# Second parts of the weights by accumulating DMAs in a hybrid decoder trunk: input projections and branch outputs

## The chip, the cores and the metric

The kernel runs on one core of one Trainium2 chip. The metric is device time in microseconds: the median of the timed runs of one program. Each execution computes one layer for 512 tokens from inputs in HBM.

## The reference

Five token mixers run side by side on one normalised input; each has its own gate path, is projected to the model width, weighted by a sigmoid gate and summed:

```python
h = rmsnorm(x, norm_g)
proj = h @ w_in + b_in                      # 1024 -> 13320, split into 19 sections
y_a = silu(layernorm(conv31(a_val * sigmoid(a_glu)))) * silu(a_z)
y_b = stick_breaking_attention(b_q, b_k, b_v) * silu(b_z)
y_c = headnorm(mlstm_chunkwise(silu(conv4(c_q, c_k)), c_v, c_i, c_f)) * sigmoid(c_o) * silu(c_z)
y_d = rg_lru(conv4(d_x)) * silu(d_z)
y_m = memory_attention(m_q, rmsnorm(mem)) * silu(m_z)
gates = sigmoid(gate_logits)                # five of 512 x 1024
merged = sum(gates[n] * (y @ w_up[n]) for n, y in enumerate((y_a, y_b, y_c, y_d, y_m)))
return rmsnorm(x + merged @ w_out, final_norm_g)
```

All is in float32; x is 512 x 1024, each branch 512 wide, the memory 256 rows.

## The kernel before, in words

**Split matmuls.** TensorE multiplies float32r operands, which hold fewer bits than float32. So each operand is kept as two parts: a first part, the value rounded to float32r (`whi`, `hH`, `yH`), and a second part, what the rounding left (`wlo`, `hL`, `yL`). `mm3` (lines 193 to 201) then makes three matmuls a term: first by first (L199), first of the weights by second of the data (L200), second of the weights by first of the data (L201). They accumulate in one PSUM bank.

**Tiling.** The normalised input stands transposed in SBUF as `hH` and `hL`, 8 blocks of 128 channels by 512 tokens. One projection (`proj`, L203) computes 128 output channels for all 512 tokens: 8 terms, 24 matmuls. Its weights are one array of 128 x 1024 float32 (512 KB), worked on in two halves of 128 x 512, one for the first four terms and one for the last four. A branch output (`up`, L963) computes 128 of 1024 model channels with 4 terms, 12 matmuls; one weight load serves two of them, so a half is again 12 matmuls.

**Two ways to make the parts.** Both load the weights from HBM into a stage tile `wst` (two buffers) by a DMA issued from SyncE. `load_w` (L149) has ScalarE copy a half into `whi` (L162) and VectorE subtract: `wlo = wst - whi` (L163; L165 and L166 with a scale). `load_w_add` (L170) has ScalarE write the rounded negative into `wlo` (L182), GpSimd issue a DMA that reads the same half of the weights from HBM again and adds it onto `wlo` (L183), and ScalarE write `whi` (L184); VectorE has no part in it. `whi` and `wlo` have six buffers each (`WHL`), so that three weight loads are held at a time. Before, the 40 gate projections (step G) use `load_w_add`; all other projections, the branch outputs, the memory's keys and values and the token-major values (`v_half`) use `load_w`.

**Order of the work.** The list `STEPS` gives the steps in program order: ac, an, ao (convolution branch), ma (memory attention), bv, bp, ba (stick-breaking attention), cv, cg, cp, ch, cn (mLSTM), ds, dt, dn (RG-LRU), G (a gate) and U (a branch output). A scheduler then orders each engine's instructions by its own estimate of durations, with weight preparation moved up (`high_priority(offset=PREP)`, 201 places). Each engine runs its instructions strictly in the order so found. Ahead of the list stands a start stage: the memory's keys and values, the norm of x and its transposes (`x_T`, L317: `hH` L321, `hL` L322), with small tiles that are given free at its end; the memsets of `kp` (L544) on GpSimd wait for that. In a stick-breaking head (`b_head`) GpSimd masks scores (L611), VectorE scans them (L618) and TensorE transposes them (L628).

Of the kernel before, what the change touches and what calls it, by code (L numbers as in the profile page):

```python
# [18 lines left out]
D = 1024  # L19
# [13 lines left out]
GATES = 8200  # L33
# [4 lines left out]
CM_INDEX = {c: i for i, c in enumerate(CM)}  # L38
# [43 lines left out]
def build(ctx, tc, x, mem, memT, cols_d, rows_d, wcm, wbv, wcv0, wcv1, wmk, wmv, wup, wout, dw, fg, out):  # L82
# [26 lines left out]
    def col(name, i):  # L109
        o = _off[name] + i  # L110
        return cols[:, o:o + 1]
# [35 lines left out]
    def f32(t):  # L147
        return t.bitcast(F32)

    def load_w(src, n, scale=None, stage=wpool):  # L150

        st = stage.tile([P, 1056], F32, tag="wst", name="wst", bufs=WST)
        nc.sync.dma_start(out=st[:, :n], in_=src)
        res = []
        m = n // 2
        for half in range(2):
            hi = wpool.tile([P, 576], F32R, tag="whi", name="whi", bufs=WHL)
            lo = wpool.tile([P, 576], F32R, tag="wlo", name="wlo", bufs=WHL)
            f = st[:, half * m:(half + 1) * m]
            with tc.high_priority(offset=PREP):  # L160
                if scale is None:
                    act(hi[:, :m], f, AF.Copy)  # L162
                    V.tensor_tensor(out=lo[:, :m], in0=f, in1=f32(hi[:, :m]), op=ALU.subtract)  # L163
                else:
                    act(hi[:, :m], f, AF.Copy, scale=scale)  # L165
                    V.scalar_tensor_tensor(out=lo[:, :m], in0=f, scalar=scale, in1=f32(hi[:, :m]),  # L166
                                           op0=ALU.mult, op1=ALU.subtract)
            res.append((hi, lo))
        return res

    def load_w_add(src, n):

        st = wpool.tile([P, 1056], F32, tag="wst", name="wst", bufs=WST)
        nc.sync.dma_start(out=st[:, :n], in_=src)
        res = []
        m = n // 2
        for half in range(2):
            hi = wpool.tile([P, 576], F32R, tag="whi", name="whi", bufs=WHL)
            lo = wpool.tile([P, 576], F32R, tag="wlo", name="wlo", bufs=WHL)
            sl = slice(half * m, (half + 1) * m)  # L180
            with tc.high_priority(offset=PREP):
                act(lo[:, :m], st[:, sl], AF.Copy, scale=-1.0)  # L182
                G.dma_start(out=lo[:, :m], in_=src[:, sl], accum_op=ALU.add)  # L183
                act(hi[:, :m], st[:, sl], AF.Copy)  # L184
            res.append((hi, lo))
        return res

    def piece(w, k, n, per, o=0, c=None):

        hi, lo = w[k // per]  # L190
        sl = slice((k % per) * n + o, (k % per) * n + (o + c if c else n))
        return hi[:, sl], lo[:, sl]


    def mm3(ps, terms, first=True, last=True, check=False):

        n = len(terms)
        for i, (ah, al, bh, bl) in enumerate(terms):
            mm(ps, lhsT=ah, rhs=bh, start=first and i == 0, stop=False, skip_group_check=check)  # L199
            mm(ps, lhsT=ah, rhs=bl, start=False, stop=False, skip_group_check=check)  # L200
            mm(ps, lhsT=al, rhs=bh, start=False, stop=last and i == n - 1, skip_group_check=check)  # L201

    def proj(c, scale=None):  # L203

        w = load_w_add(wcm[CM_INDEX[c]], D) if c >= GATES else load_w(wcm[CM_INDEX[c]], D, scale)
        ps = pj.tile([P, S], F32, tag="pj", name="pj")
        mm3(ps, [(*piece(w, k, P, 4), hH[:, k, :], hL[:, k, :]) for k in range(NK)])
        return ps, col("b_in", CM_INDEX[c])
# [179 lines left out]
    def silu_proj(c):  # L388
        ps, b = proj(c)
        z = zt()  # L390
        silu_evac(ps, b, z)
        return z

    def split_proj(c, scale=None, bias=None):
        ps, b = proj(c, scale)
        hi, lo = op_pair()
        split_evac(ps, b if bias is None else bias, hi, lo)
        return hi, lo
# [4 lines left out]
    def a_conv(i):  # L403
        ps, b = proj(A_GLU + i * P)
        sg = tpool.tile([P, S], F32, tag="sg", name="sg")
        with tc.high_priority(offset=EVAC):
            act(sg, ps, AF.Sigmoid, bias=b)
        ps, b = proj(A_VAL + i * P)
        u = apool.tile([P, 30 + S], F32, tag="u", name="u")
        V.memset(u[:, :30], 0.0)  # L410
        with tc.high_priority(offset=EVAC):
            V.scalar_tensor_tensor(out=u[:, 30:], in0=ps, scalar=b, in1=sg, op0=ALU.add, op1=ALU.mult)
        a = apool.tile([P, S], F32, tag=f"acc{i}", name=f"acc{i}", bufs=1)
        V.tensor_scalar(a, u[:, 0:S], col("a_w", i * 31), col("a_b", i), op0=ALU.mult, op1=ALU.add)
        for k in range(1, 31):
            V.scalar_tensor_tensor(out=a, in0=u[:, k:k + S], scalar=col("a_w", i * 31 + k), in1=a,  # L416
                                   op0=ALU.mult, op1=ALU.add)
        acc[i] = a
# [530 lines left out]
    upw = {}  # L949
# [13 lines left out]
    def up(n, ys):  # L963
        d = ups[n]
        ups[n] += 1
        if d % 2 == 0:
            upw[n] = load_w(wup[n, d // 2], 1024)
        g = gates[n][d]
        ps = pj.tile([P, S], F32, tag="pj", name="pj")
        mm3(ps, [(*piece(upw[n], 4 * (d % 2) + k, P, 4), *ys[k]) for k in range(NE)])  # L970
        first = d not in begun
        begun.add(d)
        with tc.high_priority(offset=EVAC):
            V.tensor_tensor(out=merged[:, d, :] if first else g, in0=g, in1=ps, op=ALU.mult)
        if not first:
            V.tensor_tensor(out=merged[:, d, :], in0=merged[:, d, :], in1=g, op=ALU.add)
# [5 lines left out]
    def step(s):  # L982
# [17 lines left out]
        elif c == "ba":  # L1000
            p = st[f"bp{i // 2}"]
            b_head(p, i % 2)
            if s[:-1] + str(i ^ 1) in st:
                ys[1][i // 2] = y_split(p[4])
            st[s] = True
        elif c == "cv":
            c_v(i)
        elif c == "cg":
            c_gates()
        elif c == "cp":  # L1010
            st[s] = c_proj(i)
        elif c == "ch":
            st[s] = c_head(st[f"cp{i}"])
        elif c == "cn":
            ys[2][2 * i:2 * i + 2] = c_norm([st[f"ch{2 * i}"], st[f"ch{2 * i + 1}"]])
        elif c == "ds":
            d_setup()
        elif c == "dt":
            st[s] = d_tile(i)
        elif c == "dn":  # L1020
            ys[3][2 * i:2 * i + 2] = d_scan([st[f"dt{2 * i}"], st[f"dt{2 * i + 1}"]])
        elif c == "G":
            gate(i)
        elif c == "U":
            assert None not in ys[i]
            up(i, ys[i])
        else:
            raise ValueError(s)
# [43 lines left out]
    for half in range(2):  # L1072
        if half:
            wo = [hl for k2 in range(4) for hl in load_out(1, k2)]
        for t in range(NT):
            tsl = slice(t * P, (t + 1) * P)
            parts = parts_of(t) if half else 1
            w = S // parts
# [96 lines left out]
```

## Time and profile before

| | before |
|---|---|
| median of 3 runs | 839.41 us (838.4 to 839.54) |
| profiled execution: its time / its span | 838.62 us / 836.6 us |
| granted TensorE clock | 0.999 |
| TensorE busy | 825.4 us (99%) |
| VectorE, ScalarE, GpSimd busy | 572.6, 490.9, 104.7 us |
| DMA | 106.33 MB, mean 127 GB/s |

The span runs from the first to the last instruction; the execution's time has 2.0 us around it. A row of the page's groups names line, engine and operation, the tiles as out<-in, the count, then busy time and mean duration, then the engine's idle time just before these instructions and what ended it. A row of waits names who waited, for whom, the total, the count and the longest. Rows of the timeline begin with start and duration. PE is TensorE, DVE VectorE, ACT ScalarE, POOL GpSimd, SP SyncE; SPq, POOLq are their queues as issuers. A matmul's recorded duration is longer than the distance to the next one, since they are pipelined; the distances are read from starts.

### The profile page before, as it was taken

Reading aid. Unit: us, or ns where it says so; the run is one execution under the profiler, and the core shown is the slowest. Engines: PE = TensorE matmul, PEld = TensorE weight load, DVE = VectorE, ACT = ScalarE, POOL = GpSimd, SP = SyncE. Lnnn points to the kernel's source line nnn. Section 1 sums busy time; section 2 is a strip of 40 time slices with the busy share of each in tenths; the row PEclk is TensorE's granted clock in tenths of the full one; section 3 lists DMA queues with packets and bytes.
Section 4 is the critical chain, followed back from the end, with each engine's and each line's share of the span. In section 5 each row is a group of like instructions: output and inputs, shape, how many; then the busy total and the mean of one; then the engine's idle time right before and its main releaser. Section 6 shows DMA issues by size and latency. Waiting matters only on the chain.

```text
span 836.6 us, 11398 instructions
## 1 busy us (share of the span) xinstructions
PE 825.4 (99%) x4064; PEld 698.0 (83%) x4064; DVE 572.6 (68%) x1098; ACT 490.9 (59%) x892; POOL 104.7 (13%) x155
## 2 busy tenths in 40 slices
PE   8999999999999999999999999999999999999996
PEld 7788888888898889788888888888888888888886
DVE  4879989997456677785676778559657564535644
ACT  6644475635545554667556546586465977884424
POOL 0000020101100232022333000010000201120000
PEclk9999999999999999999999999999999999999999
DMA  9432274345624324336624243474352645685602
GB/s 358 153 128 99 88 153 112 103 125 129 154 95 124 92 89 101 109 96 139 149 90 119 84 139 101 128 170 105 98 142 76 140 121 141 141 180 162 213 34 101
DMA packets 36240, 106.33 MB, mean 127 GB/s; under 512 B 4052, under 2 KB 4180, under 8 KB 36184
## 3 DMA queue, kind: packets, MB, share of 16 engines
q1 hardware_dynamic: 23800, 83.06, 30.0%
q0 software_dynamic: 11520, 20.98, 15.3%
q10 hardware_dynamic: 864, 1.57, 0.5%
q8 instruction: 32, 0.52, 0.3%
q14 instruction: 24, 0.20, 0.1%
HBM read 103.49 MB, written 2.11 MB: 126 GB/s over the span
## 4 chain that ended last, share of the span: by engine, by line
PE 94%; ACT 2%; DVE 1%; DMA 1%; issue 1%; SPq 0%; ACTq 0%
PE pj L201 26%; PE pj L199 26%; PE pj L200 26%; PE pj L530 2%; PE pj L528 2%; PE pj L529 2%; PE po L642 1%; PE wb L628 1%; PE og L833 1%; PE mk L286 1%; PE zb L599 1%; PE zb L598 1%; DMA mt<-in 1%; PE tp L502 0%; DVE hL L322 0%
## 5 line engine op out<-in xcount | busy, mean ns | idle before, releaser
L201 PE MATMUL pj<-hH,wlo 128*128 128x512 f32 x768 | 299.9, 391 | 0.2 <-DVE wlo L163 0.2
L200 PE MATMUL pj<-hL,whi 128*128 128x512 f32 x768 | 299.8, 390 | 0.0
L199 PE MATMUL pj<-hH,whi 128*128 128x512 f32 x768 | 299.6, 390 | 0.1
L162 ACT ACTIVATE whi<-wst 128x512 fp32r<-128x512 f32 (+1 forms) x172 | 107.1, 631 | 163.1 <-PE pj L200 118.3
L201 PEld LDWEIGHTS pj<-hH,wlo 128*128 128x128 f32 x768 | 144.2, 188 | 30.4 <-DVE wlo L163 0.7
L199 PEld LDWEIGHTS pj<-hH,whi 128*128 128x128 f32 x768 | 144.2, 188 | 29.7 <-ACT g L960 0.5
L200 PEld LDWEIGHTS pj<-hL,whi 128*128 128x128 f32 x768 | 144.3, 188 | 29.4
L163 DVE TENSOR_TENSOR wlo<-wst,whi 128x512 fp32r<-128x512 f32 (+1 forms) x172 | 117.1, 687 | 74.4 <-ACT whi L162 74.2
L183 POOL DMA_DIRECT2D wlo<-in x80 | 69.5, 869 | 559.8 <-ACT wlo L182 424.6
L416 DVE SCALAR_TENSOR_TENSOR acc<-u,cols,acc 128x512 f32<-128x512 f32 x120 | 88.7, 747 | 1.4
L184 ACT ACTIVATE whi<-wst 128x512 fp32r<-128x512 f32 x80 | 50.3, 629 | 57.1 <-PE pj L200 41.2
L200 PE MATMUL pj<-yL,whi 128*128 128x512 f32 x160 | 62.5, 390 | 0.0
L199 PE MATMUL pj<-yH,whi 128*128 128x512 f32 x160 | 62.4, 391 | 0.0
L201 PE MATMUL pj<-yH,wlo 128*128 128x512 f32 x160 | 62.3, 390 | 0.0
L182 ACT ACTIVATE wlo<-wst 128x512 fp32r<-128x512 f32 x80 | 49.4, 618 | 5.9 <-PE at L529 4.0
L201 PEld LDWEIGHTS pj<-yH,wlo 128*128 128x128 f32 x160 | 30.1, 188 | 6.2
L199 PEld LDWEIGHTS pj<-yH,whi 128*128 128x128 f32 x160 | 30.0, 188 | 6.1
L200 PEld LDWEIGHTS pj<-yL,whi 128*128 128x128 f32 x160 | 30.1, 188 | 5.9
L618 DVE TENSOR_TENSOR_SCAN kp<-kp 128x512 f32<-128x512 f32 (+3 forms) x32 | 26.9, 859 | 10.8 <-POOL kp L611 10.6
L529 PE MATMUL pj<-wlo,hH 128*128 128x256 f32 (+1 forms) x112 | 31.8, 284 | 0.0
L530 PE MATMUL pj<-whi,hL 128*128 128x256 f32 (+1 forms) x112 | 31.8, 284 | 0.0
L528 PE MATMUL pj<-whi,hH 128*128 128x256 f32 (+1 forms) x112 | 31.5, 283 | 0.0
(310 smaller groups left out, 1232.4 us busy)
## 6 DMA issues: line engine op xcount, KB each, us to landing
wst<-in SPq DMA_DIRECT2D x136, 512.0 KB, 3.4
wlo<-in POOLq DMA_DIRECT2D x80, 256.0 KB, 5.3
xt<-in SPq DMA_DIRECT2D x4, 512.0 KB, 9.0
merged<-in SPq DMA_DIRECT2D x4, 512.0 KB, 3.2
wst<-in SPq DMA_DIRECT2D x2, 528.0 KB, 4.3
mr<-in SPq DMA_DIRECT2D x2, 512.0 KB, 10.7
f<-crow SPq DMA_DIRECT2D x4, 256.0 KB, 6.6
out<-merged SPq DMA_DIRECT2D x4, 256.0 KB, 2.0
```

What stands on the lines that cost most here:

```text
L162: act(hi[:, :m], f, AF.Copy)
L163: V.tensor_tensor(out=lo[:, :m], in0=f, in1=f32(hi[:, :m]), op=ALU.subtract)
L182: act(lo[:, :m], st[:, sl], AF.Copy, scale=-1.0)
L183: G.dma_start(out=lo[:, :m], in_=src[:, sl], accum_op=ALU.add)
L184: act(hi[:, :m], st[:, sl], AF.Copy)
L199: mm(ps, lhsT=ah, rhs=bh, start=first and i == 0, stop=False, skip_group_check=check)
L200: mm(ps, lhsT=ah, rhs=bl, start=False, stop=False, skip_group_check=check)
L201: mm(ps, lhsT=al, rhs=bh, start=False, stop=last and i == n - 1, skip_group_check=check)
L416: V.scalar_tensor_tensor(out=a, in0=u[:, k:k + S], scalar=col("a_w", i * 31 + k), in1=a, op0=ALU.mult, op1=ALU.add)
L528: mm(dst[t], lhsT=hH[:, k, tsl], rhs=wh, start=first, stop=False, skip_group_check=True)
L529: mm(dst[t], lhsT=hH[:, k, tsl], rhs=wl, start=False, stop=False, skip_group_check=True)
L530: mm(dst[t], lhsT=hL[:, k, tsl], rhs=wh, start=False, stop=k == NK - 1, skip_group_check=True)
```

## The change

Two conditions. Every projection without a scale, and every branch output, now takes its weights by `load_w_add`:

```diff
     def proj(c, scale=None):
 
-        w = load_w_add(wcm[CM_INDEX[c]], D) if c >= GATES else load_w(wcm[CM_INDEX[c]], D, scale)
+        w = load_w_add(wcm[CM_INDEX[c]], D) if scale is None else load_w(wcm[CM_INDEX[c]], D, scale)
         ps = pj.tile([P, S], F32, tag="pj", name="pj")
...
         if d % 2 == 0:
-            upw[n] = load_w(wup[n, d // 2], 1024)
+            upw[n] = load_w_add(wup[n, d // 2], 1024)
         g = gates[n][d]
```

Of 56 projections that are no gates, the 4 of `B_Q` have a scale and stay; 52 change. Of branch outputs there are 40, with 20 loads. That is 72 loads or 144 halves; with the gates 112 loads are then made so. The start stage and `v_half` stay with `load_w`. The scheduler orders all engines anew.

On ScalarE, at the end of the start stage. `wlo_484` and `whi_483` are the first half of the first projection (`A_GLU`, 0), the next pair its second half; `v` is the memory's values, `hH` the last two blocks of the transposed input. Before:

```order
L217 ACTIVATE v_420<-mkf_442 128x512
L162 ACTIVATE whi_483<-wst_481 128x512
L162 ACTIVATE whi_487<-wst_481 128x512
L357 ACTIVATE v_421<-mv_151,rsq_t_426 128x512
L357 ACTIVATE v_421<-mv_152,rsq_t_426 128x512
L321 ACTIVATE hH_106<-tp_383,cols_80 128x512
```

Now:

```order
L217 ACTIVATE v_420<-mkf_442 128x512
L182 ACTIVATE wlo_484<-wst_481 128x512
L182 ACTIVATE wlo_489<-wst_481 128x512
L184 ACTIVATE whi_483<-wst_481 128x512
L184 ACTIVATE whi_488<-wst_481 128x512
L357 ACTIVATE v_421<-mv_151,rsq_t_426 128x512
L357 ACTIVATE v_421<-mv_152,rsq_t_426 128x512
L321 ACTIVATE hH_106<-tp_383,cols_80 128x512
```

Two pieces have become four, the two lo-writes first; the values and `hH` follow two places later.

On ScalarE, in the first pair of RG-LRU tiles (steps dn0 and the gates, outputs and projections around it). `whi_6733` and `whi_6737` are a branch output's weights, `whi_6758` to `whi_6800` those of the projections `D_X` and `D_Z` after it. Before:

```order
L162 ACTIVATE whi_6737<-wst_6731 128x512
L939 ACTIVATE f_6383<-f_6383 128x512
L162 ACTIVATE whi_6758<-wst_6756 128x512
L960 ACT_TABLE_LOAD
L960 ACTIVATE g_6675<-pj_6650,cols_80 128x512
L217 ACTIVATE yH_6588<-f_6577 128x512
L162 ACTIVATE whi_6762<-wst_6756 128x512
L217 ACTIVATE yH_6595<-f_6580 128x512
L162 ACTIVATE whi_6796<-wst_6794 128x512
```

Now (`whi_6862` for 6737, `whi_6884` for 6758, `whi_6889` for 6762, `whi_6924` for 6796):

```order
L184 ACTIVATE whi_6862<-wst_6855 128x512
L182 ACTIVATE wlo_6863<-wst_6855 128x512
L184 ACTIVATE whi_6884<-wst_6882 128x512
L182 ACTIVATE wlo_6885<-wst_6882 128x512
L960 ACT_TABLE_LOAD
L960 ACTIVATE g_6799<-pj_6774,cols_80 128x512
L217 ACTIVATE yH_6712<-f_6701 128x512
L217 ACTIVATE yH_6719<-f_6704 128x512
L184 ACTIVATE whi_6889<-wst_6882 128x512
L182 ACTIVATE wlo_6890<-wst_6882 128x512
L184 ACTIVATE whi_6924<-wst_6922 128x512
L182 ACTIVATE wlo_6925<-wst_6922 128x512
```

The sequence is the same, with a lo-write behind each `whi`.

On GpSimd, the masks of the third stick-breaking head. Before:

```order
L611 AFFINE_SELECT kp00_474<-kp00_474 128x128
L611 AFFINE_SELECT f_3051<-f_3051 128x128
L611 AFFINE_SELECT kp01_476<-kp01_476 128x128 x2
L611 AFFINE_SELECT f_3064<-f_3064 128x128 x2
L611 AFFINE_SELECT kp02_479<-kp02_479 128x128
```

Now, with the two DMAs of a branch output's weights inside it:

```order
L611 AFFINE_SELECT kp00_474<-kp00_474 128x128
L183 DMA wlo_3345<-in_11 128x512
L183 DMA wlo_3350<-in_11 128x512
L611 AFFINE_SELECT f_3109<-f_3109 128x128
L611 AFFINE_SELECT kp01_476<-kp01_476 128x128 x2
```

The masks after the first now wait until the two DMAs ahead of them can be issued.

## The prediction

> **What bounds the kernel now.** I read the page first (busy shares and groups), then TensorE's waits, then the groups by stretches of 20 us, then the tile `wlo`, and at last the timeline at two places. The page's first line and the list of all that TensorE waits for settle most of it:
>
> ```profile
> PE 825.4 (99%) x4064; PEld 698.0 (83%) x4064; DVE 572.6 (68%) x1098; ACT 490.9 (59%) x892; POOL 104.7 (13%) x155
> ```
>
> ```profile
> PE mk L286 <- DVE mt L274: 1.8, 2, 1.0
> PE warm L241 <- POOL ident masks.py:199: 1.4, 1, 1.4
> PE tp L320 <- DVE hL L322: 1.1, 1, 1.1
> PE pj L201 <- DVE wlo L163: 0.2, 1, 0.2
> PE mk L286 <- ACT mt L276: 0.2, 1, 0.2
> ```
>
> TensorE waits 4.7 us in all of 836.6. The change touches the origin of one of these waits: 0.2 us at the first projection. So what it takes off VectorE cannot come back as time, unless something else is hidden there; what it adds behind a matmul can cost. The costs of each step are in the groups:
>
> ```profile
> L201 PE MATMUL pj<-hH,wlo 128*128 128x512 f32 x768 | 299.9, 391 | 0.2 <-DVE wlo L163 0.2
> L162 ACT ACTIVATE whi<-wst 128x512 fp32r<-128x512 f32 (+1 forms) x172 | 107.1, 631 | 163.1 <-PE pj L200 118.3
> L163 DVE TENSOR_TENSOR wlo<-wst,whi 128x512 fp32r<-128x512 f32 (+1 forms) x172 | 117.1, 687 | 74.4 <-ACT whi L162 74.2
> L183 POOL DMA_DIRECT2D wlo<-in x80 | 69.5, 869 | 559.8 <-ACT wlo L182 424.6
> L182 ACT ACTIVATE wlo<-wst 128x512 fp32r<-128x512 f32 x80 | 49.4, 618 | 5.9 <-PE at L529 4.0
> ```
>
> and in the tile `wlo`, whose last line is min, median and max of an accumulating DMA from its issue to its landing:
>
> ```profile
> L183 POOL DMA_DIRECT2D wlo<-in x80: 844/862/1070, 105.4 to 766.1; - x80
> DMA to landing us min/median/max: 3.6/5.3/9.1
> ```
>
> **The change in numbers.** 52 projections and 20 output loads move from `load_w` to `load_w_add`: 72 loads, 144 halves. Off VectorE go 144 x 687 ns = 99 us (573 to 474). ScalarE gets 144 x 618 ns = 89 us (491 to 580, 69% of the span). GpSimd gets 144 x 869 ns = 125 us (105 to 230, 27%). Removing VectorE's work is worth nothing but the 0.2 us above. ScalarE and GpSimd stay far from full on average, so the average gives "no change"; what matters is how late a second part now is, at each place.
>
> **The delay of one half, and its cover.** Before, a second part follows its first by one VectorE instruction (0.69 us). After, it takes a ScalarE write (0.62), a step from ScalarE's end to GpSimd's issue, and 5.3 us to landing. The step is 0.3 us, from a gate of today (666.56 + 0.61 = 667.17, issue at 667.47):
>
> ```profile
> 666.56 0.61 ACT L182 ACTIVATE wlo<-wst 128x512 fp32r<-128x512 f32 x1
> ...
> 667.47 0.87 POOL L183 DMA_DIRECT2D wlo<-in  x1 [2.96 <-ACT wlo L182]
> ```
>
> So a half comes later by about 0.62 + 0.3 + 5.3 - 0.69 = 5.5 us. The cover is the ring of six halves. An ordinary stretch of 20 us (columns: PE, PEld, DVE, ACT, POOL busy, clock, DMA share, GB/s):
>
> ```profile
> 200.00:220.00 20.00, 20.00 (x90) 16.54 (x90) 11.99 (x20) 10.82 (x20) 3.42 (x4) 1.00 0.58 139
> ```
>
> TensorE does 90 matmuls in it, 0.22 to 0.23 us each; a half has 12, 2.7 us. A half may be written when its predecessor in the ring has been read, five halves (13.6 us) ahead of its first use. ScalarE does wait for exactly that release:
>
> ```profile
> ACT whi L162 <- PE pj L200: 118.3, 75, 3.6
> ACT whi L184 <- PE pj L200: 41.2, 30, 2.9
> ```
>
> With `whi` first (0.63) that leaves 13.6 - 0.63 - 0.62 - 0.3 - 5.3 = 6.8 us to spare after the change, or 3.0 with the slowest landing. So wherever ScalarE still waits for TensorE, I cost the change at nothing; the cover is this slack. It is absent in two places, and thin in a third.
>
> **First place: the first projection.** There is no ring ahead of it yet; its weights arrive as it begins.
>
> ```profile
> 34.76 1.16 ACT L162 ACTIVATE whi<-wst 128x512 fp32r<-128x512 f32 x2 [0.23 <-DMA wst<-in]
> ...
> 37.92 0.51 PE L201 MATMUL pj<-hH,wlo 128*128 128x512 f32 x1 [0.23 <-DVE wlo L163]
> ```
>
> ScalarE was held by the load itself until 34.76, which the change does not touch. By the order, `wlo_484` is now ScalarE's first piece there: done at 34.76 + 0.62 = 35.4, issued at 35.7, landed at 35.7 + 5.3 = 41.0. TensorE's order puts the first matmul with it third in the projection, as before, so it waits from 37.9 to 41.0: **+3.1 us**. Bounds with the shortest and longest landing: 39.3 (+1.4) and 44.8 (+6.9). Everything after is delayed, since nothing later has slack to give back to a TensorE that is always busy. The second half is issued 0.87 us behind, and needed 14 matmuls (3.2 us) after the first: covered. The four ScalarE pieces instead of two push `hH` for the last two terms back by 1 to 2 us; those terms now come after the stall: covered. GpSimd's `kp` memsets wait for the start stage to close,
>
> ```profile
> 39.90 0.20 POOL L544 MEMSET kp<- 128x1 f32 x4 [38.28 <-DVE v L358]
> ```
>
> and now stand ahead of the second projection's DMAs; those are issued near 40 and needed about 10 matmuls after the second half's start, near 46: just covered.
>
> [...]
>
> **Second place: ScalarE is full.** The same view, from 640 us on:
>
> ```profile
> 640.00:660.00 20.00, 20.00 (x93) 16.55 (x92) 13.98 (x23) 17.15 (x26) 2.18 (x3) 1.00 0.33 94
> 660.00:680.00 20.00, 20.00 (x90) 16.55 (x89) 9.86 (x14) 19.69 (x29) 3.02 (x4) 1.00 0.65 143
> 680.00:700.00 20.00, 20.00 (x90) 16.57 (x89) 14.22 (x23) 9.85 (x18) 1.72 (x2) 1.00 0.51 139
> ```
>
> Here ScalarE does RG-LRU's functions with their table loads, and has 0.3 us left of 20. The change adds lo-writes of 0.53 us each (the pitch: two take 1.16, less 0.63). Ahead of this stretch come six new ones, 3.2 us, against an idle time of 2.5 us:
>
> ```profile
> 647.49 0.68 ACT L920 ACTIVATE f<-dps,cols 64x512 f32<-64x512 f32 x1 [2.49 <-PE dps L919]
> ```
>
> so ScalarE enters 0.7 us late (between 0 and 2). Then, where the next projections' first parts are written today, and where their first matmul with a second part stands:
>
> ```profile
> 676.28 0.62 ACT L162 ACTIVATE whi<-wst 128x512 fp32r<-128x512 f32 x1
> ...
> 679.55 0.62 ACT L162 ACTIVATE whi<-wst 128x512 fp32r<-128x512 f32 x1
> ...
> 681.87 0.62 ACT L162 ACTIVATE whi<-wst 128x512 fp32r<-128x512 f32 x1
> ```
>
> ```profile
> 683.15 0.39 PE L201 MATMUL pj<-yH,wlo 128*128 128x512 f32 x1
> ...
> 683.83 0.39 PE L201 MATMUL pj<-hH,wlo 128*128 128x512 f32 x1
> ```
>
> The change from `yH` to `hH` marks the first half's use, 683.83; the following halves are used at 686.55 and 689.27, by 2.72 us. After the change two lo-writes stand ahead of the first of these, three ahead of the second, four ahead of the third. Their second parts land at (start + shift + 0.62 + 0.53 for its own write + 0.3 + 5.3): 676.28 + 1.06 + 6.75 = 684.1 (0.3 late); 679.55 + 1.59 + 6.75 = 687.9 (1.3 late); 681.87 + 2.12 + 6.75 = 690.7 (1.5 late). With 0.7 from ahead the worst is 2.2 us late. The stalls don't add, since each one gives the next half as much: **+2.2 us**, between 0 (an order that keeps ScalarE ahead) and 4.5 (2 us late at entry, landing 1 us slower).
>
> **Third place: the stick-breaking heads.** GpSimd masks the scores that VectorE scans, and VectorE waits for it in all eight heads:
>
> ```profile
> DVE kp L618 <- POOL kp L611: 10.6, 8, 6.0
> ```
>
> In two more heads than before a pair of accumulating DMAs now stands between the masks of one head, 2 x 0.86 = 1.7 us. Two heads already have such rows today and TensorE waits for neither, so some cover is there: +0.4 us, between 0 and 3.4.
>
> **Sum.** 3.1 + 2.2 + 0.4 = 5.7 us. The profiled execution took 838.6 us (span 836.6); that makes 844.3, and its time is 0.8 under the median of the three runs (839.4), so the median after should be **845.1 us**.
>
> **Rivals.** (1) *Nothing shows.* Landings at the low end (3.6 us) and ScalarE's order absorbing the rest. The start then costs 1.4 us, 840.8 in the median, which is within 0.2% (1.7 us, about what a measurement of this kernel can tell from no change). For it: ScalarE's 118 us of waiting, two loaded heads without a wait. Against: at the start the median landing decides and 39.3 is the earliest. It is certain only at a landing of 2.2 us (35.7 + 2.2 = 37.9), under which nothing is lost at the start. Chance 0.15, and 0.02 of it for a landing a microsecond under any of today's, 2.6 us: 0.4 us at the start and nothing later, 839.8. [...]
>
> (2) *The DMA engines become the bound.* From these rows
>
> ```profile
> q1 hardware_dynamic: 23800, 83.06, 30.0%
> q0 software_dynamic: 11520, 20.98, 15.3%
> ```
>
> an accumulating DMA takes 0.153 x 836.6 / 80 = 1.60 us of all 16 engines, a plain load of 0.524 MB 0.300 x 836.6 / 83.06 x 0.524 = 1.58. A weight then needs 1.58 + 3.20 = 4.8 us of DMA per 5.45 us of TensorE (24 matmuls of 0.227 us), 88% in every dense stretch; over the run 30 + 15.3 x 224/80 = 73%. It decides where an accumulating DMA takes over 1.93 us. At 30% longer (2.08) each of 112 weights costs 0.3 us, +34 us, 873. For it: landings up to 9.1 us today. Against: the share above already holds the contention of today. Chance 0.10.
>
> (3) *Faster.* Even if all that VectorE's waits cost TensorE after 20 us went (1.1 + 0.2), that is 1.3 us and not measurable; something unseen would be needed. Chance 0.04.
>
> My forecast has 0.71, and of it a little lies under the bound: faster 0.04, same 0.16, slower 0.80. The range takes the ends of the three terms: 1.4 above the median (840.8) to 6.9 + 4.5 + 3.4 = 14.8 above (854.2); I take 840.4 to 856, leaving the rest of rival 1 below and rival 2 above.
>
> **What would show it.** TensorE's waits should name `wlo` by DMA: one near 38 us of 2 to 4 us, a few near 684 to 692, ScalarE without idle time from 640 to 690, and no DMA share over 0.95 in whole stretches of 20 us. The groups should show L163 at x28, L182 at x224. I am wrong if TensorE does not wait at the first projection, if most of the loss comes from ordinary stretches (200 to 260 us, say), or if the landing's median passes 7 us.

## The result, and the profile after

The changed kernel took **847.62 us** (median of 3 runs, 846.35 to 847.75) against 839.41 before: a ratio of 1.0097, with a 95% interval from 1.0074 to 1.0120. That is 8.2 us slower; 845.1 was forecast, in a range from 840.4 to 856.0. The profiled execution spans 845.5 us, 8.9 more than before's 836.6.

The busy line of the page after can be held against the prediction's sums for VectorE, ScalarE and GpSimd (474, 580 and 230 us). GpSimd's holds. VectorE fell by 82 us instead of 99, and ScalarE rose by 72 instead of 89: the sums took full durations, and neighbouring instructions of one engine overlap in the rows (two lo-writes of 0.62 us take 1.15):

```profile
PE 830.5 (98%) x4064; PEld 699.4 (83%) x4064; DVE 490.2 (58%) x954; ACT 562.8 (67%) x1036; POOL 229.7 (27%) x299
```

TensorE is 5 us *busier* with the same 4064 matmuls. Part of that is matmuls that ran slower, which a list of waits cannot show. The whole list of TensorE's waits after:

```profile
PE pj L201 <- DMA wlo<-in: 4.0, 3, 2.6
PE warm L241 <- POOL ident masks.py:199: 1.4, 1, 1.4
PE tp L320 <- DVE hL L322: 1.1, 1, 1.1
PE mk L286 <- DVE mt L274: 0.8, 1, 0.8
PE pj L199 <- ACT mH L217: 0.3, 1, 0.3
PE og L833 <- ACT wlo L182: 0.2, 1, 0.2
PE mk L286 <- ACT mt L276: 0.2, 1, 0.2
PE pj L199 <- DVE g L974: 0.2, 1, 0.2
```

The 0.2 us for VectorE's `wlo` at the first projection became 4.0 us for the DMA's `wlo`, in three waits. The first, in the timeline of TensorE (start, duration, instruction, and in brackets the idle time before it):

```profile
36.84 0.40 PE L200 MATMUL pj<-hL,whi 128*128 128x512 f32 x1
39.85 0.63 PE L201 MATMUL pj<-hH,wlo 128*128 128x512 f32 x1 [2.62 <-DMA wlo<-in]
40.28 0.63 PE L199 MATMUL pj<-hH,whi 128*128 128x512 f32 x1
...
43.26 0.49 PE L200 MATMUL pj<-hL,whi 128*128 128x512 f32 x1
43.60 0.39 PE L201 MATMUL pj<-hH,wlo 128*128 128x512 f32 x1
```

From 39.85 to 43.26 the matmuls start 0.43 us apart instead of 0.23. The stretches of that time (PE, PEld, DVE, ACT, POOL busy, granted clock, DMA share, GB/s) name the reason: the clock fell behind the pause, to 0.57 from 40 to 44 us (1.00 in before).

```profile
40.00:44.00 4.00, 4.00 (x11) 3.15 (x12) 0.75 (x1) 2.61 (x6) 1.71 (x5) 0.57 0.99 206
44.00:48.00 4.00, 4.00 (x19) 3.27 (x19) 0.00 (x0) 0.60 (x2) 1.07 (x2) 1.00 1.09 249
```

The other two waits for `wlo` stand in the RG-LRU stage:

```profile
690.02 0.50 PE L201 MATMUL pj<-hH,wlo 128*128 128x512 f32 x1 [0.47 <-DMA wlo<-in]
...
694.00 0.50 PE L201 MATMUL pj<-hH,wlo 128*128 128x512 f32 x1 [0.92 <-DMA wlo<-in]
```

**Where the 8.9 us are.** Waits and slow matmuls together are seen in the distances between matmul starts. For each kernel I took from its trace the distance from each matmul to the next, less the median distance of its shape, summed by stretch of the program, less the same sum of the kernel before. The first row is after; the others are the experiments below. Each row is one execution, and not always a typical one: those of e2, e4, e6, e8 and e12 are the longest of their kernels, 0.6, 2.3, 0.8, 1.7 and 5.0 us over the median, and that of e9 is 1.1 under it.

```
us over before        0-20  20-60  60-500  500-600  600-720  720-780  780-end   sum
after                 -0.4   +4.0   -0.2     +2.1     +2.1     +0.1     +1.2    9.0
e1 first back         -0.3   +6.5   -0.1     +3.5     +0.9     +0.4     +0.3   11.3
e2 first alone        -0.2   +3.8   -0.1      0.0      0.0     +0.5      0.0    4.2
e3 ups back           -0.2   +3.8   -0.2      0.0     +3.3      0.0      0.0    6.9
e4 lo last            +1.4   +7.1   -0.2     +1.7     +2.0     +0.3     +2.4   14.8
e5 fill (+2.5 filled) +0.5   +0.2   -0.1     +1.0     +2.2      0.0     +0.6    7.0
e6 first 4 back        0.0    0.0   -0.2     +3.8     +1.8     +0.2     +1.4    7.1
e7 forty               0.0    0.0   -0.2      0.0      0.0     +0.3      0.0    0.1
e8 ScalarE alone      -0.3    0.0   +0.5     +2.0     +4.0     +0.7      0.0    7.1
e9 VectorE, first 4   -0.2    0.0   -0.1     -0.1     +2.2     +0.4     +1.5    3.9
e10 VectorE negates   +1.4   +7.4   -0.1     -0.1     +4.5     +0.3     +2.4   15.9
e11 most               0.0    0.0   -0.1     +0.3     +0.4     +0.2      0.0    1.0
e12 most, ScalarE      0.0    0.0   -0.1     +7.2     +2.0      0.0      0.0    9.2
```

The last column is of the whole program (it holds what the rounded columns leave). After loses at four places: the start (4.0), the mLSTM heads at 500 to 600 us (2.1), the RG-LRU stage (2.1) and the tail (1.2). Between 60 and 500 us, where 76 of the 144 new lo-writes stand, it loses nothing.

The rest of the signs. The groups show the move as forecast (L182 and L183 x224, L163 x28). The DMA's share should have stayed under 0.95 in whole stretches of 20 us; it is over that in three of them:

```profile
L182 ACT ACTIVATE wlo<-wst 128x512 fp32r<-128x512 f32 x224 | 138.4, 619 | 17.0 <-PE pj L529 7.7 <-DMA wst<-in 5.2 <-PE at L529 4.0
L183 POOL DMA_DIRECT2D wlo<-in x224 | 195.1, 878 | 526.8 <-ACT wlo L182 492.3 <-ACT rr L838 11.7 <-ACT sg L223 5.7
L163 DVE TENSOR_TENSOR wlo<-wst,whi 128x512 fp32r<-128x512 f32 (+1 forms) x28 | 18.7, 687 | 15.5 <-ACT whi L162 15.4
```

```profile
40.00:60.00 20.00, 20.00 (x82) 16.36 (x83) 7.32 (x11) 12.35 (x21) 8.14 (x11) 0.91 1.02 226
60.00:80.00 20.00, 20.00 (x96) 16.78 (x95) 18.56 (x29) 10.09 (x17) 5.72 (x7) 1.00 1.02 214
...
760.00:780.00 20.00, 20.00 (x90) 16.56 (x89) 5.17 (x8) 10.15 (x18) 6.06 (x7) 1.00 1.05 250
```

and the tile `wlo` gives the way of an accumulating DMA from issue to landing, 5.3 us in the median before:

```profile
DMA to landing us min/median/max: 3.6/5.8/8.9
```

The plain loads became slower too: a weight load of 512 KB lands 5.2 us after its issue in the median, 3.4 before.

### The profile page after: what moved, and what is told of

It is laid out like the page before. It is cut to its first block, busy times and chain, and to the rows that moved or that the text cites. A ratio compares the mean times of both kernels' runs of the same rounds, so it can differ in the third digit from the quotient of the medians.

```text
span 845.5 us, 11696 instructions
## 1 busy us (share of the span) xinstructions
PE 830.5 (98%) x4064; PEld 699.4 (83%) x4064; DVE 490.2 (58%) x954; ACT 562.8 (67%) x1036; POOL 229.7 (27%) x299
## 3 DMA queue, kind: packets, MB, share of 16 engines
q0 software_dynamic: 32256, 58.73, 41.8%
q1 hardware_dynamic: 23800, 83.06, 31.7%
HBM read 141.24 MB, written 2.11 MB: 170 GB/s over the span
## 4 chain that ended last, share of the span: by engine, by line
PE 82%; ACT 5%; issue 5%; DMA 4%; DVE 2%; POOL 1%; SPq 0%; POOLq 0%; ACTq 0%
PE pj L199 23%; PE pj L201 23%; PE pj L200 23%; PE pj L528 2%; PE pj L530 2%; PE pj L529 2%; DMA f<-crow 2%; DMA wlo<-in 1%; PE po L642 1%; DMA wst<-in 1%; PE wb L628 1%; ACT whi L184 1%; ACT wlo L182 1%; POOL wlo L183 1%; PE mk L286 1%
## 5 line engine op out<-in xcount | busy, mean ns | idle before, releaser
L183 POOL DMA_DIRECT2D wlo<-in x224 | 195.1, 878 | 526.8 <-ACT wlo L182 492.3
L184 ACT ACTIVATE whi<-wst 128x512 fp32r<-128x512 f32 x224 | 140.3, 629 | 141.9 <-PE pj L200 89.7
L182 ACT ACTIVATE wlo<-wst 128x512 fp32r<-128x512 f32 x224 | 138.4, 619 | 17.0 <-PE pj L529 7.7
L974 DVE TENSOR_TENSOR g<-g,pj 128x512 f32<-128x512 f32 x32 | 21.8, 681 | 31.9 <-PE pj L201 31.8
L529 PE MATMUL pj<-wlo,hH 128*128 128x256 f32 (+1 forms) x112 | 31.7, 284 | 0.0
L530 PE MATMUL pj<-whi,hL 128*128 128x256 f32 (+1 forms) x112 | 31.7, 284 | 0.0
L528 PE MATMUL pj<-whi,hH 128*128 128x256 f32 (+1 forms) x112 | 31.7, 284 | 0.0
L751 DVE TENSOR_SCALAR f<-u,cols 128x512 f32<-128x512 f32 x12 | 6.8, 564 | 36.2 <-ACT u L746 21.1
```

Source lines behind the costliest of these rows:

```text
L528: mm(dst[t], lhsT=hH[:, k, tsl], rhs=wh, start=first, stop=False, skip_group_check=True)
L529: mm(dst[t], lhsT=hH[:, k, tsl], rhs=wl, start=False, stop=False, skip_group_check=True)
L530: mm(dst[t], lhsT=hL[:, k, tsl], rhs=wh, start=False, stop=k == NK - 1, skip_group_check=True)
```

## The experiments

Two theories stood at the beginning. *Local*: the time is lost at a few places where a second part has no lead. *Traffic everywhere*: 144 more accumulating DMAs slow all transfers, and the loss goes with their number. Medians below are of 4 to 11 runs, each beside runs of the kernel before on the same chip (838.78 to 839.14 in the median).

### The start: first projection given back (e1), alone (e2), reordered (e4), pause filled (e5), first four given back (e6)

e1 edits line 205 of the kernel after:

```diff
-        w = load_w_add(wcm[CM_INDEX[c]], D) if scale is None else load_w(wcm[CM_INDEX[c]], D, scale)
+        w = load_w_add(wcm[CM_INDEX[c]], D) if scale is None and c != A_GLU else load_w(wcm[CM_INDEX[c]], D, scale)
```

> The kernel after, with the first projection's weights (both halves) split by VectorE again; the other 70 changed loads stay. Local theory (9 us lost at five places, of which 4.2 at the first projection: a wait of 2.6 us for the accumulating DMA, then nine matmuls at half clock, 0.2 us more each): the wait and the half clock both go, 847.6 - 4.2 = 843.4 us, granted clock 1.00 from 40 to 44 us. Rival, traffic everywhere (the loss is spread over the 224 accumulating DMAs through slower landings): two of 224 change, 847.5 us. Rival on the clock (the half clock comes from something else than the pause): the wait goes and the dip stays, 847.6 - 2.4 = 845.2 us.

Measured: **849.71 us** (845.07 to 851.59), 1.0117 (1.0094 to 1.0140). Both theories miss the median; the local one named 843.4. Two of the six executions took 845.1 and 845.8 us; the traced one took 850.3. The wait did go from the first projection, and came back larger at the second:

```profile
37.61 0.50 PE L201 MATMUL pj<-hH,wlo 128*128 128x512 f32 x1 [0.25 <-DVE wlo L163]
47.27 0.79 PE L201 MATMUL pj<-hH,wlo 128*128 128x512 f32 x1 [3.92 <-DMA wlo<-in]
```

and GpSimd's timeline shows when that projection's DMAs were issued, at 38.41 us:

```profile
38.41 1.89 POOL L183 DMA_DIRECT2D wlo<-in  x2 [36.79 <-DVE wlo L163]
```

Its first half was issued when the first projection had just begun and landed 8.8 us later. In the kernel after, the pause and the slow matmuls behind it delay the need for this half to 46.6 us; with them gone the need comes about 3.4 us earlier. The landing itself also took longer here, 8.8 us against 5.9 for the same half in after.

e2 edits the same line of the kernel before:

```diff
-        w = load_w_add(wcm[CM_INDEX[c]], D) if c >= GATES else load_w(wcm[CM_INDEX[c]], D, scale)
+        w = load_w_add(wcm[CM_INDEX[c]], D) if c >= GATES or c == A_GLU else load_w(wcm[CM_INDEX[c]], D, scale)
```

> The kernel before, with only the first projection's second parts by accumulating DMAs. Local theory: the whole cost of the start without anything else, a wait of 2.5 to 3.1 us and the half clock behind it, 839.4 + 4.2 = 843.6 us. Rival, traffic everywhere: 839.5 us, not to be told from before. Rival on the clock: the wait alone, 839.4 + 2.4 = 841.8 us.

Measured: **842.22 us**, 1.0036 (1.0024 to 1.0048), 3.4 us more than before; its trace has 3.8 at the start (the wait and the half clock) and 0.5 at most anywhere else. The start's whole cost needs only these two DMAs of the 144 new ones, which speaks against traffic everywhere. Two of the five executions, 841.1 and 841.3 us at a mean granted clock of 0.999, lie 2.3 and 2.6 us over before, about what the longer wait alone costs; the other three, at 0.995 to 0.997, lie 3.4 to 4.0 over it. So the half clock may follow the pause in some executions only. That isn't shown, as only one of them was traced.

e4 puts the first projection's eight `wlo` matmuls behind its sixteen others (a helper `mm3_last` in place of `mm3` for `A_GLU`):

```diff
+def mm3_last(mm, ps, terms):
+    n = len(terms)
+    for i, (ah, al, bh, bl) in enumerate(terms):
+        mm(ps, lhsT=ah, rhs=bh, start=i == 0, stop=False)
+        mm(ps, lhsT=ah, rhs=bl, start=False, stop=False)
+    for i, (ah, al, bh, bl) in enumerate(terms):
+        mm(ps, lhsT=al, rhs=bh, start=False, stop=i == n - 1)
```

> The kernel after, with the first projection's eight matmuls on second parts put behind its sixteen on first parts; nothing else differs. Local theory: TensorE has 14 or more matmuls (3.2 us) to do while the accumulating DMA is under way, so neither the wait nor the half clock remains: 847.6 - 4.2 = 843.4 us. Rival, traffic everywhere: 847.6 us. Rival on the clock: 845.2 us with the clock at about 0.57 from 40 to 44 us all the same. A new wait could come for hH of the last terms or for the first parts of the second half, up to 1.5 us.

Measured: **851.12 us**, 1.0140 (1.0125 to 1.0155). The same thing in another way: TensorE had work while the first half came, reached the second projection's `wlo` early, and waited 3.5 us there (7.1 us at the start with the half clock). Its trace also has 1.4 us more before 20 us, where the clock fell during the first transfers (0.73 from 10 to 14 us, against 1.00 in before); e10's trace loses the same 1.4 there. What set that off is open.

e5 repeats the first matmul of the first projection eleven times; each repetition starts the sum anew:

```diff
+        [mm(ps, lhsT=w[0][0][:, :P], rhs=hH[:, 0, :], start=True, stop=True) for _ in range(11 * (c == A_GLU))]
```

> The kernel after, with the first projection's first matmul done eleven more times ahead of itself (each starts the sum anew, so the last one counts): 2.5 us of useless work where TensorE stood idle for 2.6 us. If the half clock behind the pause comes from the pause, the granted clock is 1.00 from 36 to 44 us, the wait for wlo at the first projection is under 0.5 us, and the nine matmuls behind it take 0.23 instead of 0.43 us each: 1.8 us less; some of it is lost again, since the second half and the second projection had 1.2 and 0.7 us to spare in the neighbouring kernels: 847.6 - 1.8 + 0.7 = 846.5 us, between 845.8 and 848. If the half clock comes from something else, it stays at about 0.57 and the time is 847.6 us or more.

Measured: **845.82 us**, 1.0083 (1.0069 to 1.0097), 7.0 over before against after's 8.2, with the repeated matmuls in it. The stretches show TensorE busy through the pause and the clock whole:

```profile
36.00:40.00 4.00, 4.00 (x23) 3.41 (x22) 3.59 (x6) 4.00 (x9) 2.06 (x5) 1.00 0.81 211
40.00:44.00 4.00, 4.00 (x17) 2.77 (x16) 1.06 (x4) 3.71 (x8) 2.61 (x5) 1.00 1.01 207
```

Useless work in place of idle time takes the half clock away at this place (1.00 from 40 to 44 us, 0.57 in after), as the theory of the pause says. The start then costs 0.2 + 11 x 0.227 = 2.7 us instead of 4.0.

e6 splits the first four projections on VectorE (a counter of the projections without a scale):

```diff
-        w = load_w_add(wcm[CM_INDEX[c]], D) if scale is None else load_w(wcm[CM_INDEX[c]], D, scale)
+        w = load_w_add(wcm[CM_INDEX[c]], D) if scale is None and counted() > 4 else load_w(wcm[CM_INDEX[c]], D, scale)
```

> The kernel after, with the first four projections (not one) split by VectorE. In the kernel before, VectorE's second parts were 0.1, 2.3, 2.0, 4.1, 5.9, 8.0, 7.3 us ahead of their first use in the first seven halves and over 9 us after that. Ring theory (what counts is how far ahead of its use a half is written; an accumulating DMA takes 5.5 to 8.5 us more of that lead here): with the first eight halves left to VectorE no projection starts without lead, no wait for wlo by DMA before 600 us, no half clock at 40 to 60 us, 847.6 - 4.2 = 843.4 us. Rival, DMA engines: they are at 0.95 to 1.05 of their time from 38 to 80 us whichever projection begins, so the stall moves on to the fifth projection as it moved on to the second one: 847 us or more, with a wait for wlo near 60 us.

Measured: **844.89 us**, 1.0068 (1.0054 to 1.0081). The start's loss is 0.0 in the trace, with no wait for `wlo` there: four projections of lead are enough. The DMA engines as a bound of the start fell with this. The total is 1.5 above the expected one because the mLSTM heads lose 3.8 here instead of 2.1.

### Behind the start: output loads given back (e3), forty projections (e7), ScalarE's work alone (e8)

e3 edits line 967 of the kernel after:

```diff
-            upw[n] = load_w_add(wup[n, d // 2], 1024)
+            upw[n] = load_w(wup[n, d // 2], 1024)
```

> The kernel after, with the 20 output loads split by VectorE again; the 52 projections stay. Local theory: the 4.2 us at the start stay; of the other 4.8 (mLSTM heads 2.0, RG-LRU stage about 1.7, tail 1.2) the tail's 1.2 goes with the last output loads, and the RG-LRU stage loses some of the lo-writes ahead of it: 847.6 - 1.2 - 1.0 = 845.4 us, between 844 and 847. Rival, traffic everywhere: 40 of 144 new DMAs go, 847.6 - 9 x 40/144 = 845.1 us, with the wait at the first projection unchanged; here the two do not differ by time, only by place: the local theory has no gap of TensorE left from 780 us on and all of 0 to 60 us.

Measured: **845.16 us**, 1.0074 (1.0060 to 1.0087). Nothing is lost in the mLSTM heads or at the tail; the start keeps its 3.8; the RG-LRU stage loses 3.3, more than in after and not less as expected: TensorE waits 1.4 us there for ScalarE's gate and 1.3 us for a `wlo` by DMA.

e7 gives back the first four projections, `D_X` and `D_Z`, and the output loads (e3's edit with this one):

```diff
+        w = load_w_add(wcm[CM_INDEX[c]], D) if scale is None and counted() > 4 and not D_X <= c < M_Q else load_w(wcm[CM_INDEX[c]], D, scale)
```

> The kernel after, with the first four projections, the eight of the RG-LRU inputs (D_X, D_Z) and the 20 output loads split by VectorE: 40 of the 72 changed loads, 80 of the 144 new accumulating DMAs, stay. Ring theory (all that is lost is lost at the few places without lead): 839.4 us, between 838.5 and 841.0, not to be told from before. Rival, traffic everywhere: the loss goes with the number of DMAs, 8.2 x 80/144 = 4.6 us over before, 844.0 us.

Measured: **838.50 us**, 0.9994 (0.9985 to 1.0003): no difference from before, with 80 new accumulating DMAs and as many new writes of ScalarE. TensorE's waits hold no `wlo` by DMA any more:

```profile
PE warm L241 <- POOL ident masks.py:199: 1.4, 1, 1.4
PE tp L320 <- DVE hL L322: 1.1, 1, 1.1
PE mk L286 <- DVE mt L274: 0.9, 2, 0.4
PE pj L201 <- DVE wlo L163: 0.2, 1, 0.2
PE mk L286 <- ACT mt L276: 0.2, 1, 0.2
```

Traffic everywhere is out as a cost that goes with the number of DMAs. What is left is which of the two new things, ScalarE's write or the DMA's landing, costs at each place.

e8 adds ScalarE's write to the kernel before, in the 72 loads, and no DMA:

```diff
                 if scale is None:
+                    if extra: act(lo[:, :m], f, AF.Copy, scale=-1.0)
                     act(hi[:, :m], f, AF.Copy)
```

> The kernel before, with ScalarE's negated write into the second part added to the 72 loads (VectorE then overwrites it with the difference): the 89 us more of ScalarE's work without any new DMA and without a longer way for the second part. If the losses behind the start come from ScalarE's queue: about 2 us in the mLSTM heads near 585 us, about 2 in the RG-LRU stage near 690 us and the tail's 1.2 near 795 us come back, 839.4 + 4 = 843.5 us or so. If they come from the landing of the DMAs: 839.4 us, within 0.8 us. Neither says that the start loses more than 1 us here.

Measured: **843.62 us**, 1.0056 (1.0043 to 1.0069). ScalarE's writes alone cost 4.8 us in the median. The traced execution is the longest of five (845.3) and loses 7.1: in the mLSTM heads (2.0) and above all in the RG-LRU stage (4.0), where TensorE waits for the evacuation of a gate that stands behind them on ScalarE (line 961 here is 960 of before):

```profile
688.03 0.54 PE L200 MATMUL pj<-hH,whi 128*128 128x512 f32 x1 [1.82 <-ACT g L961]
```

About 1.7 of these 4.0 us are half clock behind that pause: the next matmuls start 0.43 us apart until 691.8. The tail loses nothing.

### The DMAs without ScalarE's writes (e9, e10), and the pair that closes the account (e11, e12)

e9 and e10 let VectorE write the negated first part of the changed loads; e9 also gives back the first four projections with e6's counter:

```diff
-                act(lo[:, :m], st[:, sl], AF.Copy, scale=-1.0)
+                V.tensor_scalar_mul(lo[:, :m], st[:, sl], -1.0) if neg else act(lo[:, :m], st[:, sl], AF.Copy, scale=-1.0)
```

> The kernel after, with the first four projections split by VectorE and, in the other 68 changed loads, the negated first part written by VectorE in place of ScalarE: the new accumulating DMAs (136 of 144) and their late landing are all there, ScalarE's 89 us more are not. Queue theory (behind the start, ScalarE's queue costs the time, not the landing): 838.8 us like before, within 840.5; no gap of TensorE near 515, 585, 690 and 795 us. Landing theory (late second parts and the traffic cost it): 844.9 us, as in the kernel with only the first four projections given back.

Measured: **843.27 us** (840.46 to 844.91), 1.0046 (1.0031 to 1.0062). Neither theory: the mLSTM heads are whole again (-0.1), but the RG-LRU stage loses 2.2 and the tail 1.5 without any new write of ScalarE. In the RG-LRU stage it is one wait:

```profile
688.32 0.50 PE L201 MATMUL pj<-hH,wlo 128*128 128x512 f32 x1 [1.88 <-DMA wlo<-in]
```

VectorE negated that half at 680.4, behind work of its own, and its DMA took from 681.1 to 688.3, so a queue ahead of the DMA has a part in it here too. The matmuls behind this pause ran at the full clock, although it is as long as e8's. At the tail the chain reads back from TensorE to VectorE, to ScalarE, to a plain load. TensorE and VectorE:

```profile
789.94 0.50 PE L199 MATMUL pj<-woH,mH 128*128 128x512 f32 x1 [1.22 <-DVE g L974]
```

```profile
787.99 1.30 DVE L1051 TENSOR_TENSOR woL<-wst,woH 128x512 fp32r<-128x512 f32 x2 [3.64 <-ACT woH L1050]
789.20 0.68 DVE L974 TENSOR_TENSOR g<-g,pj 128x512 f32<-128x512 f32 x1
```

and ScalarE:

```profile
787.33 1.15 ACT L1050 ACTIVATE woH<-wst 128x512 fp32r<-128x512 f32 x2 [3.22 <-DMA wst<-in]
```

The output projection's weights come late, their split stands ahead of a gate's product on VectorE, and that product frees the PSUM buffer that TensorE wants. A reason for the late load can be read from the stretch from 760 to 780, first of e9 and then of e7, which has no accumulating output loads:

```profile
760.00:780.00 20.00, 20.00 (x90) 16.57 (x89) 10.64 (x19) 8.51 (x15) 5.25 (x6) 1.00 0.96 223
```

```profile
760.00:780.00 20.00, 20.00 (x90) 16.54 (x89) 13.81 (x23) 9.96 (x18) 1.72 (x2) 1.00 0.62 174
```

The DMA engines are full in e9 (0.96, and in after 1.05) where the last accumulating output loads meet the loads of the output projection; the first of these took 6.5 us to land in e9 and 5.6 in e7. Kernels without those last accumulating loads (e3, e7, e11) lose nothing at the tail.

> The kernel after, with the negated first part of all 72 changed loads written by VectorE: the start's accumulating DMAs are there, ScalarE's 89 us more are not. Queue theory: the start alone is lost, as in the kernel before with only the first projection changed, 838.8 + 3.4 to 4.2 = 842.6 us, between 842 and 843.5. Landing theory: 847 us, as after.

Measured: **852.92 us** (849.22 to 856.58), 1.0157 (1.0131 to 1.0183): worse than both theories allow. At the start VectorE's negations stand ahead of the split of `hL`, and TensorE waits twice, with the half clock behind:

```profile
42.13 0.47 PE L199 MATMUL pj<-hH,whi 128*128 128x512 f32 x1 [3.06 <-DVE hL L322]
...
45.13 0.79 PE L201 MATMUL pj<-hH,wlo 128*128 128x512 f32 x1 [2.30 <-DMA wlo<-in]
```

The mLSTM heads are whole (-0.1) as in e9; the RG-LRU stage (4.5, a wait of 2.5 us for `wlo` and half clock behind it) and the tail (2.4, a wait of 2.1 us for VectorE's `g`) lose more than in e9. Why these waits are longer stays open.

e11 keeps VectorE's negation and gives back what e6 to e9 point at: the first four projections, `D_X` and `D_Z`, and the output loads of the RG-LRU branch, which are the last.

```diff
+        w = load_w_add(wcm[CM_INDEX[c]], D, c < GATES) if scale is None and counted() > 4 and not D_X <= c < M_Q else load_w(wcm[CM_INDEX[c]], D, scale)
...
+            upw[n] = load_w_add(wup[n, d // 2], 1024) if n != 3 else load_w(wup[n, d // 2], 1024)
```

> The kernel after, with VectorE splitting the first four projections, the eight RG-LRU inputs and the four output loads of the RG-LRU branch (the last ones), and VectorE writing the negated first part of the other 56 changed loads: 112 of the 144 new accumulating DMAs stay, none of ScalarE's new writes. Place theory (accumulating DMAs cost only where the lead is short or the DMA engines are full: start, RG-LRU stage, tail; ScalarE's writes cost in the mLSTM heads): 839.1 us like before, within 1 us. Rival, traffic everywhere: 839.1 + (843.3 - 839.1) x 112/136 = 842.6 us.

Measured: **838.88 us**, 0.9999 (0.9991 to 1.0008): 112 of the 144 new accumulating DMAs cost nothing that can be measured.

e12 is e11 with ScalarE writing the negated parts (`neg=False`).

> The same kernel, with ScalarE writing the negated first part, as after does: the difference is 112 writes of ScalarE and nothing in the DMAs. Place theory: the mLSTM heads lose their 2 us (1.2 to 4.1 us between 500 and 600 us in the neighbouring kernels), the rest nothing: 839.1 + 2 = 841 us, between 840 and 843. If ScalarE's writes cost nothing by themselves: 839.1 us.

Measured: **842.59 us**, 1.0045 (1.0032 to 1.0059), 3.7 more for 112 writes of ScalarE. The main place is the mLSTM heads again; there ScalarE's writes push VectorE's operands of the heads back (VectorE waits 1.63 us for ScalarE's `op` at 513 us). The RG-LRU stage loses 2.0 as well, which was not expected. The execution that was profiled took 847.5, the longest of six, so its 7.2 and 2.0 us are more than the median's. TensorE at the main place:

```profile
515.54 0.71 PE L833 MATMUL og<-v,op 128*128 128x258 f32 x4 [0.85 <-DVE op L816]
...
518.46 0.69 PE L834 MATMUL og<-v,op 128*128 128x130 f32 x2 [0.88 <-DVE op L817]
...
521.82 0.63 PE L201 MATMUL pj<-hH,wlo 128*128 128x512 f32 x1
522.25 0.63 PE L199 MATMUL pj<-hH,whi 128*128 128x512 f32 x1
```

**A row that comes late in the mLSTM heads.** Each head loads a row of its decays, `crow`, by SyncE, the engine that also issues the weight loads, each of which waits there until a stage buffer is free (in after 449.5 us, in 89 waits, for ScalarE's `wlo` alone). SyncE ahead of the third head's row, before and then after:

```profile
540.19 13.33 SPq L174 DMA_DIRECT2D wst<-in  x3
553.57 0.42 SPq L787 DMA_DIRECT2D f<-crow  x1
```

```profile
543.83 20.95 SPq L174 DMA_DIRECT2D wst<-in  x4
564.87 0.38 SPq L787 DMA_DIRECT2D f<-crow  x1
```

Four weight loads stand ahead of the row instead of three. In after VectorE then waits for the row, and a little later for ScalarE's `rr`, which stands behind a lo-write:

```profile
570.79 1.14 DVE L797 SCALAR_TENSOR_TENSOR f<-f,acol,cmask 128x128 f32<-128x128 f32 x4 [3.02 <-DMA f<-crow]
575.92 0.17 DVE L841 TENSOR_TENSOR rr<-rr,em 128x4 f32<-128x4 f32 x1 [1.71 <-ACT rr L838]
```

```profile
575.22 0.62 ACT L182 ACTIVATE wlo<-wst 128x512 fp32r<-128x512 f32 x1
575.74 0.15 ACT L838 ACTIVATE rr<-og 128x1 f32<-128x1 f32 x1
```

The row lands 11.9 us ahead of that head's first `og` matmul, and 17.8 before. All kernels that lose a microsecond or more from 560 to 600 us (after, e1, e4, e5, e6, e8, e12) have four loads there and 11 to 12 us, all others three and 17 to 18. So an order that the scheduler chose for SyncE goes with the loss, and no run separates it from the time of ScalarE's writes.

No version beats the kernel before: e7 and e11 end at its time, since TensorE is 99% busy there and all that the change gives free is VectorE's.

## Why the prediction was right, and where it was not

The sign, two of the four places and the reason at them held: no gain from a VectorE that nobody waits for, and second parts that are late where the ring has no lead. Point by point:

- **First projection, +3.1: right in kind, 4.0 in size.** `wlo_484` was issued at 35.40 (35.7 forecast) and TensorE could go on at 39.85 (41.0), so the landing was 4.4 and not 5.3; the pause grew by 2.4. The missing part is the clock, which the prediction had at nothing: about 1.7 us, eight matmuls at 0.43 us and one at 0.34. e5 showed that it hangs on the pause. A landing 0.9 us too long and a missing 1.7 us partly cancel, so that the term is as near as it is by luck.
- **"Covered" for the second half of the first projection: only just.** It landed at 43.6, 3.8 us behind the first and not 0.9, and was used at 44.8. The 14 matmuls between take 3.2 us at full speed, so the half clock helped to cover it; in e5, at full clock, it landed 0.05 us ahead of its use.
- **"Just covered" for the second projection: held in after, and hid a loss.** In after its first half lands at 45.2 and is used at 46.6, so 1.4 us are to spare, in a start that had already lost 4.0. e1 and e4 uncovered it: 3.9 and 3.5 us of wait. The terms of this start don't add; the largest shadows the next, and removing it pays out that one.
- **Ordinary stretches, 0: right.** -0.2 us between 60 and 500 us, and e7 and e11 show it with 80 and 112 DMAs. Rival 2 as a bound of the whole (873) is out; its DMA share of 73% over the run came true (41.8 and 31.7%).
- **RG-LRU stage, +2.2: measured 2.1,** with 1.7 of it at 690.0 and 694.0, the first two of the three halves named, and ScalarE without a gap from 652 to 690. But the reason was half told: e8 (only ScalarE's writes, no new DMA) waits 1.8 us there for a gate, and e9 (the DMAs, without ScalarE's writes) 1.9 us for a second part, so each can cost this by itself.
- **Stick-breaking heads, +0.4: 0** (-0.2 from 60 to 500 us).
- **Not foreseen: the mLSTM heads, +2.1.** The failed step is "wherever ScalarE still waits for TensorE, I cost the change at nothing". It looked only at when the second part is ready. What is late here is not a weight but the heads' own operands, for which VectorE waits: on ScalarE behind its added writes, and for the decay row behind one more weight load on SyncE. e9 and e11, without these writes, lose nothing there (0.3 at most); e8 and e12, with them, do. e3 loses nothing with the 104 writes of the projections, and e7 with 80, so of ScalarE's writes it takes those of the output loads.
- **Not foreseen: the tail, +1.2.** The failed step is rival 2, weighed as a bound of all 112 weights: its 88% of a dense stretch counts these weights alone, and no share over 0.95 was expected in any stretch. The share is 1.05 from 760 to 780, where other loads meet them, and the loss there is a microsecond. That the full engines cause it is read from e9's chain and the kernels that lose nothing, not shown by itself.
- **Rival 1's landing of 2.6 us: not shown.** The shortest landing was 3.6 us in both traces, of 80 before and of 224 after, and the first half of the first projection took 4.4 in after.

The sum: 5.7 forecast; +0.9 at the start, -0.1, -0.6 between 60 and 500, +2.1, +1.2, and -0.3 in the rest of the table make 8.9.

## What to carry to other kernels

When a step of a load path becomes a longer one, list the places where its lead is shorter than the new way, and for each engine that gets work also list who else stands in its queue there; the average busy share says nothing of either. Loads on SyncE have a queue too: here four weight loads held SyncE for 20.95 us ahead of the third mLSTM head's row, in before three for 13.33. A stall at the start can hide the ones behind it: before taking credit for its removal, work out the next one. And where TensorE is always busy, a pause can cost more than its length (here 1.7 us more, behind 2.6).

## What the runs showed of the hardware

A pause of 2.6 us (after) or 2.4 us (e2) of a busy TensorE was followed by 3.4 us of matmuls at 0.43 instead of 0.23 us, a granted clock of 0.57 over 40 to 44 us; after 3.9 us of pause (e1) it lasted 4.9 us. In e12 it came without a single long pause: two gaps of 0.85 and 0.88 us, among short matmuls, were followed by half clock from 518.5 to 525:

```profile
515.00:520.00 5.00, 3.45 (x17) 3.04 (x18) 4.56 (x11) 3.77 (x7) 1.72 (x2) 0.83 0.78 165
520.00:525.00 5.00, 5.00 (x15) 4.03 (x15) 4.84 (x23) 1.60 (x8) 0.86 (x1) 0.50 0.83 163
```

Nor did the length decide alone in these runs: 3.4 us of half clock followed 1.82 us of pause in e8, and none followed 1.88 us in e9 or 2.11 us in e10 (at the tail).

An accumulating DMA of 256 KB landed in 3.6 us at the least of 224 in after, as of the 80 in before; the medians are 5.8 and 5.3 us. Between 40 and 60 us, where the DMA share was 1.02 in after, it took 5.2 to 8.5 us (in e1 up to 10.2, and 8.8 for the half that it waits for).
